# All stores of h on GpSimd, two h loads ahead of the last stores, and another order of splits at the head of a block

## The chip, the cores and the metric

The kernel runs on one core of one Trainium2 chip. The metric is the device time of one execution in microseconds. In the profile PE is TensorE, DVE is VectorE, ACT is ScalarE, POOL is GpSimd and SP is SyncE, which here only issues transfers.

## The reference

One decoder layer over 512 tokens of width 2048: two groups of attention heads, a cross attention to 256 memory tokens, and a SwiGLU. The change lies in the last part alone, with D_FF = 5632:

```python
hf = rms_norm(x, g_ffn)
gg, uu = jnp.split(hf @ w_gu, 2, axis=-1)
return x + (jax.nn.silu(gg) * uu) @ w_down
```

Below, h is `silu(gg) * uu`.

## The kernel before, in words

All matrix products run in fp32 accuracy on a reduced-precision matmul: each operand is split into a high part, a rounded copy (ScalarE, `S.copy`), and a low part, the rest (VectorE, `tensor_sub`), and a product is three matmuls (`mm3`: high x high, high x low, low x high). `split` (its line in the profile is L159 for both halves) is used for weights and activations alike. TensorE's matmuls are recorded on L99.

Both projections of the SwiGLU use a scheme with seven products instead of eight for a 2x2 block matrix, so weights and activations are also added and subtracted before they are split.

**Up projection.** Eleven blocks n of 512 columns of D_FF (`NB` = 11). In a block, phase 1 computes four of the products and phase 2 three; each phase goes over eight pairs of K tiles (kp = 0 to 7). For each kp, `weights_1` (phase 1) loads `raw` through SP, subtracts (L1288), splits the first 1024 columns ("a"), adds (L1290), keeps a copy of the sum in a `T4` tile (L1292), and splits the other 1024 columns ("b"). In phase 1 TensorE takes the products of pairs 0 and 1 first, product by product: the first two products use halves of b, the next two use a; then pair by pair. All splits are buffered in five `qh` and four `ql` tiles, the loads in three `raw` tiles.

**h.** When block n is done, h of block n-1 is turned while phase 2 of block n runs (`turn`): for each of two halves k, `blocks` transposes 32x32 squares on VectorE into one `T4` tile (L1390), `combine` adds and subtracts into a second (L1398 to L1401), and two `put` store them to HBM in runs of 128 bytes, eight DMAs each (L1410). So a block has 32 stores and uses four `T4` tiles, and there are four `T4` buffers. For blocks 0 to 9 all stores are issued by GpSimd. For the last block, 10, `turn` runs in step 0 of the down projection, and its stores are issued in turn by SP and by ScalarE:

```python
if step == 0 and kp in (2, 4):
    for i, go in enumerate(turn(hs, NB - 1, kp // 2 - 1)):
        go(*[(nc.sync, nc.scalar)] if i > 1 else [])
```

**Down projection.** Four steps with one or two products each; in a step 22 kp. h is loaded back through GpSimd (`load_h`, L1554) in six groups of two blocks (the last of one), into `PB` tiles, and split into two more `PB` tiles. There are 16 `PB` buffers; until the last phase 2 they hold the activations of the up projection and come free kp by kp. Group g serves kp 4g to 4g+3. In step 0, groups 0 to 3 are loaded ahead of the loop, group 4 is written at kp 5 and group 5 (block 10 alone) at kp 11; the loads of groups 2 and 3 wait for a chosen matmul of the last phase 2 (`gate`). Weights come through SP into `raw`, two kp at a time (`load_w`). In step 0 the residual x, stored before, is also loaded into `raw` and turned back by TensorE (`turn_x2`, L1622) behind the odd kp from 5 on; ScalarE copies it out of PSUM (L1625), half of it into two `T4` tiles for each of two halves.

**Order.** The program is written in one sequence; a scheduler makes from it one queue for each engine, by priorities (`high_priority` moves an instruction ahead by so many places, `AHEAD` = 150, `EVICT` = 170) and by what its own model says is ready. On the chip each engine then works its queue strictly in order. A DMA is an entry in the queue of the engine that issues it; where it must wait for a buffer or an earlier transfer, everything behind it in that queue waits too. Work handed to `phase` in `extra` is written behind the named kp of the phase.

Of the kernel before, what the change touches and what calls it, by code (L numbers as in the profile page):

```python
# [25 lines left out]
NB = D_FF // 512  # L26
# [34 lines left out]
def hybrid_block(ctx: ExitStack, tc: tile.TileContext, x_t, mem_t, sv, cmat, umask, w_a, w_r67, w_v, w_vg, w_v3,  # L61
# [94 lines left out]
    def split(hi, lo, src, gain=None):  # L156

        if gain is None:
            return S.copy(hi, src), V.tensor_sub(lo, src, hi)  # L159
        return (S.activation(hi, src, AF.Copy, scale=gain),  # L160
                V.scalar_tensor_tensor(lo, src, gain, hi, op0=OP.mult, op1=OP.subtract))
# [45 lines left out]
    def part(pair, a, n):  # L207
        return pair[0][:, a:a + n], pair[1][:, a:a + n]
# [879 lines left out]
    def sb1(tag, dt=F32):  # L1088
        return pool1.tile([128, COLS2.get(tag, 512)], dt, name=tag, tag=tag, bufs=BUFS2[tag])
# [7 lines left out]
    def split_cols(raw, a, n):  # L1097
        hi, lo = sb1("qh", F32R), sb1("ql", F32R)
        done_split[0] = split(hi[:, :n], lo[:, :n], raw[:, a:a + n])
        return hi, lo  # L1100
# [91 lines left out]
    def sb2(tag, dt=F32):  # L1192
        return pool2.tile([128, COLS2.get(tag, 512)], dt, name=tag, tag=tag, bufs=BUFS2[tag])
# [86 lines left out]
    def keep(kp):  # L1280
        if kp % 2 == 0:
            t = sb1("T4")
            kept[kp], kept[kp + 1] = t[:, :512], t[:, 512:]

    def weights_1(n, kp):
# [7 lines left out]
        b = split_cols(raw, 1024, 1024)  # L1293
        return part(b, 512, 512), part(b, 0, 512), part(a, 0, 512), part(a, 512, 512)

    def weights_2(n, kp):
        raw = sb1("raw")
        nc.sync.dma_start(raw[:, :1024], w_gu[n, kp, :, 0:1024])
        V.tensor_sub(raw[:, 1024:1536], raw[:, 0:512], kept[kp])
        a = split_cols(raw, 0, 1024)  # L1300
        b = split_cols(raw, 1024, 512)
        return part(a, 0, 512), part(b, 0, 512), part(a, 512, 512)
# [46 lines left out]
    PHASE_1 = (4, 0, 5, 3)  # L1349
    PHASE_2 = (1, 2, 6)  # L1350

    def phase(load, banks, plan, middle, last, fresh, ahead, extra, fence=()):

        ws = {}

        def weights(kp):
            with tc.high_priority(offset=AHEAD if kp > 1 else ahead), ExitStack() as behind:
                if kp == 2:
                    for i in fence:
                        behind.enter_context(tc.issue_after(i.ins))  # L1360
                ws[kp] = load(kp)

        for kp in range(2):
            weights(kp)
        for p, a in enumerate(plan):
            for kp in range(2):
                product(banks[p], kp, a, ws[kp][p], fresh and kp == 0, False, not fresh)
        for kp in range(2, KP):
            weights(kp)
            for p in last if kp == KP - 1 else middle:  # L1370
                product(banks[p], kp, plan[p], ws[kp][p], False, kp == KP - 1, not fresh)
            for go in extra.get(kp, ()):
                go()
# [77 lines left out]
    def late_sum():  # L1451
        return {kp: [sums.pop(0)] for kp in (3, 5)}

    rc2 = []
    gate = []
    hs = None
    fence = ()
    for n in range(NB):
        if n == 0:
            b1, bp = first_banks  # L1460
            u, c11 = [sb2("C") for _ in range(2)], [sb2("C") for _ in range(2)]
            with tc.high_priority(offset=2 * EVICT):
                for i in range(2):
                    fa = S.copy(u[i], b1[i])
                for i in range(2):
                    fv = V.tensor_add(c11[i], u[i], bp[i])
            bu, b2, b3 = [bank("mm"), bank("mm")], [bank("mm"), bank("o")], [bank("t"), bank("t")]

            def last_sums():
                with tc.high_priority(offset=AHEAD):  # L1470
                    with tc.issue_after(splits_b[1][0].ins), tc.issue_after(splits_b[1][1].ins):
                        form_sums(KP - 1)

            phase(lambda kp: weights_b(n, kp), (bu, b2, b3), (4, 5, 3), (1, 2, 0), (0, 1, 2), True, 40,
                  {2: [last_sums]}, (fa, fv))
        else:
            b1 = c11 = [bank("mm"), bank("mm")]
            bu = [bank("s"), bank("s")]
            b2 = [bank("t"), bank("t")]
            b3 = [bank("mm"), bank("o")]  # L1480
            phase(lambda kp: weights_1(n, kp), (bu, b1, b2, b3), PHASE_1, (2, 3, 1, 0), (1, 0, 2, 3), True, AHEAD, late_sum(),
                  fence)
            u = [sb2("C") for _ in range(2)]
        c22 = [sb2("C") for _ in range(2)]
        with tc.high_priority(offset=EVICT):
            for i in range(2):
                if n:
                    fa = S.copy(u[i], b1[i])
                V.tensor_add(u[i], u[i], bu[i])
            for i in range(2):  # L1490
                V.tensor_add(c22[i], u[i], b2[i])  # L1491
            for i in range(2):
                fv = V.tensor_add(c22[i], c22[i], b3[i])
        extra = {}
        if hs:
            one, two = [turn(hs, n - 1, k) for k in range(2)]
            extra = {2: [one[0]], 3: [one[1], one[2]], 4: [one[3]], 5: [two[0]], 6: [two[2], lambda: gate.append(last_mm[0])],
                     7: [two[1], two[3]]}
            if ready_made:
                extra[5] += [ready_made.pop(0), ready_made.pop(0)]  # L1500
        if n == 0:
            def scales():
                ss2 = sb2("C")
                G.dma_start(ss2, ssd)
                rc2.append(token_norm_col(ss, D, NT, ss2))

            phase(lambda kp: weights_c(n, kp), (b2, b3), (2, 6), (0, 1), (0, 1), False, AHEAD, {3: [scales]}, (fv,))
            rc2 = rc2[0]
        else:
            phase(lambda kp: weights_2(n, kp), (b1, b2, b3), PHASE_2, (1, 0, 2), (0, 1, 2), False, AHEAD, extra,  # L1510
                  (fa, fv))
        g1, g2 = [sb2("C") for _ in range(2)], [sb2("C") for _ in range(2)]
        with tc.high_priority(offset=EVICT):
            for i in range(2):
                fa = S.activation(g1[i], c11[i], AF.Silu, scale=rc2[:, i:i + 1])
            for i in range(2):
                V.tensor_add(g2[i], u[i], b2[i])  # L1517
            for i in range(2):
                fv = V.tensor_add(u[i], u[i], b3[i])
        fence = fa, fv  # L1520
        for i in range(2):
            S.activation(g2[i], g2[i], AF.Silu, scale=rc2[:, 2 + i:3 + i])
        for i in range(2):
            V.scalar_tensor_tensor(g1[i], u[i], rc2[:, i:i + 1], g1[i], op0=OP.mult, op1=OP.mult)
        for i in range(2):
            V.scalar_tensor_tensor(g2[i], c22[i], rc2[:, 2 + i:3 + i], g2[i], op0=OP.mult, op1=OP.mult)
        hs = g1 + g2

    STEPS = ((6,), (0, 3), (4, 5), (1, 2))
    quad = [(i, j) for i in range(2) for j in range(2)]
    groups, dw = {}, {}

    SPLIT_AT = {(1, 3): (1, 6)}
    for s in (1, 2, 3):
        SPLIT_AT[s, 4], SPLIT_AT[s, 5] = (s, 10), (s, 14)
        if s > 1:
            SPLIT_AT[s, 0], SPLIT_AT[s, 1], SPLIT_AT[s, 2], SPLIT_AT[s, 3] = (s - 1, 18), (s, 2), (s, 4), (s, 6)
    h_raw = {}  # L1540

    def split_h(step, g):
        n = 512 * len(GRP[g])
        for a in STEPS[step]:
            hi, lo = sb2("PB", F32R), sb2("PB", F32R)
            split(hi[:, :n], lo[:, :n], h_raw.pop((a, g))[:, :n])
            groups[a, g] = hi, lo

    def load_h(step, g):
        n = 512 * len(GRP[g])  # L1550
        for a in STEPS[step]:
            raw = h_raw[a, g] = sb2("PB")
            r = 128 * SLOT[a] - 128
            i = G.dma_start(raw[:, :n], hd[g][r:r + 128])  # L1554
            if step == 0 and g in (2, 3):
                tc.add_manual_dep(i.ins, gate[-1].ins.name,
                                  mybir.DependencyInfo(mybir.DependencyClass.Sync, mybir.DependencyReason.DATA),
                                  reason="in its turn")
        if (step, g) not in SPLIT_AT:
            split_h(step, g)  # L1560

    def late_splits(step, kp):
        for (s, g), at in SPLIT_AT.items():
# [87 lines left out]
    SETS = ("mm", "o", "t", "t"), ("s", "s", "mm", "mm")  # L1651
    banks = [None, [bank(t) for t in SETS[1]]]

    for g in range(len(GRP) - 2):
        load_h(0, g)
    for step, plan in enumerate(STEPS):
        rs_ = range(len(plan))
# [8 lines left out]
        for kp in range(NK):  # L1666
# [18 lines left out]
                        nc.sync.dma_start(raw, x2d[m // 4])  # L1685
                    turned[step, kp] = turn_x2(m, raw)
            if step == 0 and kp in (2, 4):
                for i, go in enumerate(turn(hs, NB - 1, kp // 2 - 1)):
                    go(*[(nc.sync, nc.scalar)] if i > 1 else [])
            if step == 0 and kp in (5, 11):  # L1690
                load_h(0, len(GRP) - (2 if kp == 5 else 1))
            if step < 3 and kp % 4 == 3:
# [139 lines left out]
```

## Time and profile before

| | |
|---|---|
| median of 3 timed runs | 2299.12 us (2298.78 to 2301.11) |
| profiled execution: its own time | 2295.67 us |
| its span, first to last instruction | 2293.6 us |
| granted TensorE clock, mean | 0.997 |
| up projection, blocks 1 to 10, one block | about 77 us |
| down projection | from 1845 us to the end |

Times within the profile are microseconds from the span's start. A row of the timeline is start, duration, engine, line, operation, output <- inputs, shapes, count, and in brackets the idle time before it and what ended that idle time. A row of the waits is engine, line and tensor <- what it waited for: microseconds in total, times, longest. A row of a window is its bounds and length, then for each engine the busy time and its instructions, then the granted clock, the busy share of the DMA engines and GB/s. A row of a DMA queue is packets, MB, and the share of 16 engines over the window; a row of DMA issues ends with KB each and the microseconds to landing.

### The profile page before, as it was taken

How to read it: one execution, taken by the hardware profiler on the slowest of the kernel's cores; microseconds unless marked ns; L12 is line 12 of the kernel's file. 1: busy time of each engine (PE TensorE's matmuls, PEld its weight loads, DVE VectorE, ACT ScalarE, POOL GpSimd, SP SyncE). 2: the span in 40 equal slices, each digit the busy share in tenths (PEclk: the TensorE clock that was granted, in tenths of full speed). 3: DMA queues.
4: the chain of work that ended last, by engine and by line, in shares of the span. 5: the costliest groups of instructions: out<-in, count | busy, mean ns of one | idle time of the engine just before them, and what ended most of it. 6: DMA issues, size and time to landing. Idle time of an engine off the chain costs nothing.

```text
span 2293.6 us, 29822 instructions
## 1 busy us (share of the span) xinstructions
PE 2264.0 (99%) x10597; PEld 1876.0 (82%) x10597; DVE 1687.8 (74%) x2643; ACT 1163.7 (51%) x1811; POOL 365.6 (16%) x560
## 2 busy tenths in 40 slices
PE   9999999999999999999999999999999979999999
PEld 7988888888888888787888888888888868888887
DVE  6478766677784446698888888988898856775685
ACT  6334545566774345675445444544454436444452
POOL 0012100011110000110223322332233220000000
PEclk9999999999999999999999999999999989999999
DMA  6577656466654334685556656665665588766754
GB/s 197 142 184 183 171 156 172 123 174 174 164 170 168 135 132 138 219 231 178 181 176 206 196 174 182 206 190 174 182 212 175 166 275 302 266 233 249 266 206 147
DMA packets 144565, 434.21 MB, mean 189 GB/s; under 512 B 33024, under 2 KB 34048, under 8 KB 140960
## 3 DMA queue, kind: packets, MB, share of 16 engines
q1 hardware_dynamic: 88176, 307.75, 39.7%
q0 software_dynamic: 44064, 115.12, 20.7%
q10 hardware_dynamic: 12176, 9.44, 1.3%
q8 instruction: 83, 1.36, 0.2%
q14 instruction: 66, 0.54, 0.1%
HBM read 390.81 MB, written 94.11 MB: 211 GB/s over the span
## 4 chain that ended last, share of the span: by engine, by line
PE 89%; DVE 5%; DMA 3%; issue 2%; ACT 1%; DVEq 0%; SPq 0%; POOL 0%; ACTq 0%
PE mm L99 49%; PE t L99 16%; PE s L99 14%; PE o L99 9%; DVE ql L159 2%; DMA raw<-w_gu 1%; PE t L817 1%; DMA h<-T 1%; DVE wl L159 1%; DMA raw<-w_down 0%; DVE C L1517 0%; ACT qh L159 0%; DMA w<-w_vsw 0%; DMA w<-w_c 0%; ACT wh L159 0%
## 5 line engine op out<-in xcount | busy, mean ns | idle before, releaser
L159 ACT CAST qh<-raw 128x1024 fp32r<-128x1024 f32 (+1 forms) x526 | 512.5, 981 | 523.1 <-PE o L99 143.4
L159 DVE TENSOR_TENSOR ql<-raw,qh 128x1024 fp32r<-128x1024 f32 (+1 forms) x526 | 589.0, 1128 | 142.1 <-PE mm L99 51.3
L99 PE MATMUL mm<-X,wh 128*128 128x512 f32 x1600 | 504.1, 395 | 0.0
L99 PEld LDWEIGHTS mm<-X,wh 128*128 128x128 f32 x1600 | 294.0, 188 | 56.4 <-issue 0.8
L99 PE MATMUL t<-qh,PB 128*128 128x512 f32 x968 | 333.4, 389 | 0.0
L99 PE MATMUL mm<-X,wl 128*128 128x512 f32 x800 | 313.6, 392 | 0.5 <-DVE wl L159 0.4
L99 PE MATMUL mm<-qh,PB 128*128 128x512 f32 x868 | 310.2, 390 | 1.8 <-DVE C L1491 0.9
L159 DVE TENSOR_TENSOR wl<-w,wh 128x1024 fp32r<-128x1024 f32 (+2 forms) x150 | 179.6, 1199 | 154.2 <-ACT wh L159 152.4
L159 ACT CAST wh<-w 128x1024 fp32r<-128x1024 f32 (+2 forms) x150 | 154.3, 1030 | 239.5 <-PE mm L99 179.5
L99 PE MATMUL s<-qh,PB 128*128 128x512 f32 x672 | 233.4, 392 | 14.4 <-ACT PB L159 14.3
L1410 POOL DMA_DIRECT2D h<-T x320 | 204.2, 708 | 217.1 <-DVE T L1390 174.4
L99 PE MATMUL mm<-qh,PA 128*128 128x512 f32 x640 | 221.4, 389 | 0.0
L99 PEld LDWEIGHTS t<-qh,PB 128*128 128x128 f32 x968 | 181.7, 188 | 38.1 <-ACT qh L159 0.2
L99 PEld LDWEIGHTS mm<-qh,PB 128*128 128x128 f32 x868 | 163.1, 188 | 37.1 <-ACT qh L159 2.1
L99 PE MATMUL t<-ql,PB 128*128 128x512 f32 x484 | 188.3, 389 | 0.0
L99 PE MATMUL o<-qh,PB 128*128 128x512 f32 x484 | 187.4, 389 | 0.0
L99 PEld LDWEIGHTS mm<-X,wl 128*128 128x128 f32 x800 | 150.3, 188 | 33.0 <-DVE wl L159 1.9
L99 PE MATMUL mm<-ql,PB 128*128 128x512 f32 x434 | 169.3, 390 | 0.0
L99 PEld LDWEIGHTS s<-qh,PB 128*128 128x128 f32 x672 | 126.4, 188 | 40.9 <-ACT PB L159 14.6
L99 PEld LDWEIGHTS mm<-qh,PA 128*128 128x128 f32 x640 | 120.1, 188 | 25.0
L99 PE MATMUL s<-ql,PB 128*128 128x512 f32 x336 | 132.7, 395 | 4.4 <-DVE ql L159 4.2
L99 PE MATMUL mm<-ql,PA 128*128 128x512 f32 x320 | 124.5, 389 | 0.0
(495 smaller groups left out, 3513.4 us busy)
## 6 DMA issues: line engine op xcount, KB each, us to landing
raw<-w_gu SPq DMA_DIRECT2D x88, 768.0 KB, 4.8
raw<-w_gu SPq DMA_DIRECT2D x88, 512.0 KB, 3.9
raw<-w_down SPq DMA_DIRECT2D x84, 512.0 KB, 4.7
td<-w_down POOLq DMA_DIRECT2D x66, 512.0 KB, 6.4
w<-w_a SPq DMA_DIRECT2D x60, 512.0 KB, 4.4
raw<-td SPq DMA_DIRECT2D x22, 1024.0 KB, 4.8
PB<-h POOLq DMA_DIRECT2D x35, 512.0 KB, 5.5
w<-w_out SPq DMA_DIRECT2D x32, 512.0 KB, 3.5
```

Source lines behind the costliest of these rows:

```text
L99: last_mm[0] = PE.matmul(*args, **kw)
L159: return S.copy(hi, src), V.tensor_sub(lo, src, hi)
L817: PE.transpose(tp[:, 128 * (i - j):128 * (i - j) + 128], ps_[b][:, POFF[i] + 128 * j:POFF[i] + 128 * j + 128], ident)
L1410: queues[i].dma_start(rows[:, :, c:c + 32], src[32 * q:32 * q + 32, :, i])
```

## The change

Three edits.

1. The stores of block 10 go through the default of `put`, GpSimd, as those of the other blocks do.
2. The loads and splits of h groups 0 and 1 for step 0 move from ahead of the down projection into phase 2 of the last block: group 0 ahead of the `combine` and the first store behind kp 3, group 1 ahead of the next `blocks` behind kp 5. The definitions of `load_h` and what it uses move up for that.
3. In blocks 1 to 10 the first two pairs of phase 1 are loaded and split by one new function: both loads, then for each pair the subtraction, the addition, the kept copy and the split of b, and only then the splits of a for both pairs.

```diff
+    def first_weights(n):
+        raws, a, b = [sb1("raw") for _ in range(2)], [], []
+        for kp, raw in enumerate(raws):
+            nc.sync.dma_start(raw[:, :1536], w_gu[n, kp, :, 512:2048])
+        for kp, raw in enumerate(raws):
+            V.tensor_sub(raw[:, 0:1024], raw[:, 0:1024], raw[:, 512:1536])
+            V.tensor_add(raw[:, 1536:2048], raw[:, 0:512], raw[:, 1024:1536])
+            keep(kp)
+            S.copy(kept[kp], raw[:, 1536:2048])
+            b.append(split_cols(raw, 1024, 1024))
+        for raw in raws:
+            a.append(split_cols(raw, 0, 1024))
+        return [(part(b[i], 512, 512), part(b[i], 0, 512), part(a[i], 0, 512), part(a[i], 512, 512)) for i in range(2)]
...
-        for kp in range(2):
-            weights(kp)
+        if both:
+            with tc.high_priority(offset=ahead):
+                ws.update(enumerate(both()))
+        else:
+            for kp in range(2):
+                weights(kp)
...
             phase(lambda kp: weights_1(n, kp), (bu, b1, b2, b3), PHASE_1, (2, 3, 1, 0), (1, 0, 2, 3), True, AHEAD, late_sum(),
-                  fence)
+                  fence, lambda: first_weights(n))
...
             extra = {2: [one[0]], 3: [one[1], one[2]], 4: [one[3]], 5: [two[0]], 6: [two[2], lambda: gate.append(last_mm[0])],
                      7: [two[1], two[3]]}
+            if n == NB - 1:
+                extra[3].insert(0, lambda: load_h(0, 0))
+                extra[5].insert(0, lambda: load_h(0, 1))
...
-    for g in range(len(GRP) - 2):
+    for g in range(2, len(GRP) - 2):
         load_h(0, g)
...
             if step == 0 and kp in (2, 4):
-                for i, go in enumerate(turn(hs, NB - 1, kp // 2 - 1)):
-                    go(*[(nc.sync, nc.scalar)] if i > 1 else [])
+                for go in turn(hs, NB - 1, kp // 2 - 1):
+                    go()
```

More of the change, by code (lines that the diff above doesn't have):

```diff
@@ L1350, in hybrid_block, with phase @@
     PHASE_2 = (1, 2, 6)
-    def phase(load, banks, plan, middle, last, fresh, ahead, extra, fence=()):
+    def phase(load, banks, plan, middle, last, fresh, ahead, extra, fence=(), both=None):
         ws = {}
@@ L1452, in late_sum, with split_h, load_h @@
         return {kp: [sums.pop(0)] for kp in (3, 5)}
+    STEPS = ((6,), (0, 3), (4, 5), (1, 2))
+    quad = [(i, j) for i in range(2) for j in range(2)]
+    groups, dw = {}, {}
+    SPLIT_AT = {(1, 3): (1, 6)}
+    for s in (1, 2, 3):
+        SPLIT_AT[s, 4], SPLIT_AT[s, 5] = (s, 10), (s, 14)
+        if s > 1:
+            SPLIT_AT[s, 0], SPLIT_AT[s, 1], SPLIT_AT[s, 2], SPLIT_AT[s, 3] = (s - 1, 18), (s, 2), (s, 4), (s, 6)
+    h_raw = {}
+    def split_h(step, g):
+        n = 512 * len(GRP[g])
+        for a in STEPS[step]:
+            hi, lo = sb2("PB", F32R), sb2("PB", F32R)
+            split(hi[:, :n], lo[:, :n], h_raw.pop((a, g))[:, :n])
+            groups[a, g] = hi, lo
+    def load_h(step, g):
+        n = 512 * len(GRP[g])
+        for a in STEPS[step]:
+            raw = h_raw[a, g] = sb2("PB")
+            r = 128 * SLOT[a] - 128
+            i = G.dma_start(raw[:, :n], hd[g][r:r + 128])
+            if step == 0 and g in (2, 3):
+                tc.add_manual_dep(i.ins, gate[-1].ins.name,
+                                  mybir.DependencyInfo(mybir.DependencyClass.Sync, mybir.DependencyReason.DATA),
+                                  reason="in its turn")
+        if (step, g) not in SPLIT_AT:
+            split_h(step, g)
     rc2 = []
@@ L1527, in hybrid_block @@
         hs = g1 + g2
[L1531 to L1560, printed above, removed]
     def late_splits(step, kp):
```

## The prediction

> **What bounds the kernel now.** First I read the page's totals, to see which engine fills the time:
>
> ```profile
> span 2293.6 us, 29822 instructions
> ...
> PE 2264.0 (99%) x10597; PEld 1876.0 (82%) x10597; DVE 1687.8 (74%) x2643; ACT 1163.7 (51%) x1811; POOL 365.6 (16%) x560
> ```
>
> TensorE (PE) is busy 99%, and the change adds or removes no matmul. What it can win are waits of PE; what it can lose are new ones. So next come PE's waits, from 1200 us to the end and then for 1100 to 1850 alone:
>
> ```profile
> PE s L99 <- ACT PB L159: 14.3, 1, 14.3
> PE s L99 <- DVE ql L159: 4.2, 8, 1.1
> ```
>
> ```profile
> PE s L99 <- DVE ql L159: 4.0, 7, 1.1
> ```
>
> So one long wait, for a ScalarE split of h, and seven short ones at the block boundaries (4.0 us together). PE's timeline shows where the long one lies:
>
> ```profile
> 1850.42 0.39 PE L99 MATMUL s<-qh,PB 128*128 128x512 f32 x1
> ...
> 1853.14 0.39 PE L99 MATMUL s<-qh,PB 128*128 128x512 f32 x1
> ...
> 1855.87 1.04 PE L1622 MATMUL t<-ident,raw 128*128 128x128 f32 x8
> 1871.23 0.79 PE L99 MATMUL s<-qh,PB 128*128 128x512 f32 x1 [14.33 <-ACT PB L159]
> ...
> 1875.99 0.40 PE L99 MATMUL s<-qh,PB 128*128 128x512 f32 x1
> ```
>
> Step 0 of the down projection takes 2.72 us for each kp (1850.42 to 1853.14, 12 matmuls). kp 0 to 3 use h group 0 and run; kp 4 needs group 1 and waits 14.33 us. The 12 matmuls from 1871.23 to 1875.99 then take 4.76 us, 2.04 more than 2.72. Why group 1 is late is seen in ScalarE's timeline, SP's, GpSimd's (POOL) and the chain of waits, in this order:
>
> ```profile
> 1856.96 13.13 ACTq L1410 DMA_DIRECT2D h<-T  x11
> 1870.14 1.04 ACT L159 CAST PB<-PB 128x1024 fp32r<-128x1024 f32 x1 [13.37 <-DMA h<-T]
> ```
>
> ```profile
> 1856.63 16.62 SPq L1410 DMA_DIRECT2D h<-T  x16
> 1873.34 0.46 SPq L1685 DMA_DIRECT2D raw<-x  x1
> ```
>
> ```profile
> 1822.16 0.64 POOL L1410 DMA_DIRECT2D h<-T  x1 [1.94 <-DVE T L1390]
> ...
> 1846.31 2.69 POOL L1410 DMA_DIRECT2D h<-T  x4 [1.09 <-DMA h<-T]
> 1849.47 0.57 POOL L1554 DMA_DIRECT2D PB<-h  x1 [0.47 <-issue]
> ```
>
> ```profile
> 1852.33 7.02 DMA raw<-w_down
> ...
> 1859.37 8.46 DMA h<-T
> ...
> 1867.85 2.30 DMA h<-T
> ```
>
> Group 1 was requested at 1849.47, behind block 9's 32 stores. But ScalarE, which must split it, stands from 1856.96 to 1870.14 in 11 stores of block 10's h, each held back by earlier transfers. The blocked ScalarE, not the data, holds PE.
>
> **The change part by part.**
>
> *Stores of block 10 go to POOL.* ScalarE loses 16 issues and SP 16. Group 1's load was issued at 1849.47 and lands by this row:
>
> ```profile
> PB<-h POOLq DMA_DIRECT2D x1, 512.0 KB, 6.5
> ```
>
> That is 1856.0; one cast (1.04) gives 1857.0, against 1856.9, when PE wants it. So this part alone recovers nearly all of the 14.33 us, and the 2.04 us of slow matmuls with it. SP is also free for the second x tile from 1856.63 instead of 1873.34.
>
> The price is on POOL. Each store costs there what these rows say (minimum, median, maximum ns):
>
> ```profile
> L1410 POOL DMA_DIRECT2D h<-T x320: 615/649/1107, 1129.8 to 1848.3; - x160
> ...
> L1410 SPq DMA_DIRECT2D h<-T x16: 302/346/515, 1856.6 to 1872.7; - x16
> ```
>
> 32 x 0.649 = 20.8 us of issue; with its waits, the set of block 9 took 1822.16 to 1849.00 = 26.8 us. VectorE's first transposes for block 10 end at 1856.93:
>
> ```profile
> 1855.84 1.09 DVE L1390 STREAM_TRANSPOSE T<-C 128x256 f32<-128x256 f32 x3
> ```
>
> So the last store is issued at about 1883.7 and has landed 4.2 us later (next row, the page's) at 1887.9:
>
> ```profile
> h<-T POOLq DMA_DIRECT2D x160, 64.0 KB, 4.2
> ```
>
> Queued behind the stores on POOL are h groups 4 and 5 of step 0. Group 5 needs all stores of block 10: 1887.9 + 6.5 + a split of under 2.3 = 1896.7; kp 20 wants it at 1856.9 + 16 x 2.72 + 7 x 1.04 (sets of transposes) = 1907.7. Hidden, with 11 us to spare. Group 4: 1883.7 + 6.5 + 2.3 = 1892.5 against kp 16 at 1856.9 + 12 x 2.72 + 5 x 1.04 = 1894.7. Hidden, by only 2 us; every microsecond beyond that would be PE's. Step 1's h loads behind them are wanted after 1907 and have more.
>
> On the DMA engines the POOL stores are no dearer: GpSimd's queue in 1745 to 1773, a stretch with 32 stores, and ScalarE's in 1845 to 1876, with 16:
>
> ```profile
> q0 software_dynamic: 975, 1.77, 25.1%
> ```
>
> ```profile
> q10 hardware_dynamic: 6889, 0.85, 18.7%
> ```
>
> 28 x 0.251 = 7.0 us of all engines for 32 against 31 x 0.187 = 5.8 us for 16.
>
> *What is late next.* Two waits come up once PE runs on. The first: the four T4 buffers. Block 10's stores read four T4 tiles, and the residual copies of the first x tile (kp 5) want two more, which must come free by stores landing. Before, VectorE met such a wait:
>
> ```profile
> 1868.41 0.43 DVE L1398 TENSOR_TENSOR T<-T 128x256 f32<-128x256 f32 x1 [7.71 <-DMA h<-T]
> ```
>
> On POOL the first two tiles are stored by 16 issues from 1856.93: 10.4 us at 0.649, 13.4 at the pace of block 9's set; plus 4.2 they free T4 at 1871.5 to 1874.5. PE's transposes of kp 7 come at 1856.9 + 4 x 2.72 = 1867.8 and need the PSUM banks that those copies empty. If the copies stand in ScalarE's queue for T4, PE waits 3.7 to 6.7 us, and the splits behind the copies with it; if other instructions are queued ahead, 0. The second: kp 10's weights need the raw buffer that the x tile holds until those transposes, as SP's own wait shows:
>
> ```profile
> SPq L1574 <- PE t L1622: 11.2, 1, 11.2
> ```
>
> The order of these two is the same before and after, and before it cost PE nothing that matters; only a slower landing does. w_down's landing was 4.8 us in 1878 to 1886, 8.2 in 1850 to 1857:
>
> ```profile
> raw<-w_down SPq DMA_DIRECT2D x2, 512.0 KB, 4.8
> ```
>
> ```profile
> raw<-w_down SPq DMA_DIRECT2D x2, 512.0 KB, 8.2
> ```
>
> So 0 to 3.4 us. A gap of PE also slows the matmuls after it, 0 to 2.04 us. Give-back: 0 to 6.7 + 3.4 + 2.0 = 12.1. I take 5.0, the middle of the T4 wait and nothing for the rest, since the nearest row is VectorE's 7.71 in the same place.
>
> The granted clock in that gap (column after the busy times):
>
> ```profile
> 1865.00:1870.00 5.00, 0.00 (x0) 0.00 (x0) 1.52 (x4) 0.00 (x0) 0.00 (x0) 0.50 0.77 123
> ```
>
> [...]
>
> *The first two h loads ahead of block 9's last stores.* Two POOL issues move ahead and push those stores by 2 x 0.57 = 1.1 us; nobody waits for them but group 4. Group 0 was split inside phase 2 already; new there is group 1's split, 1.04 us on ScalarE and some 1.2 on VectorE. Phase 2's last 30 us, and the following stretch, by engine:
>
> ```profile
> 1815.00:1845.00 30.00, 30.00 (x134) 24.82 (x134) 24.66 (x40) 15.36 (x19) 17.85 (x29) 1.00 0.80 249
> 1845.00:1876.00 31.00, 16.63 (x70) 13.05 (x69) 18.72 (x31) 9.35 (x16) 6.04 (x11) 0.78 0.99 275
> ```
>
> VectorE has 5.3 us idle and ScalarE 14.6 there; without that cover 1.2 us would be PE's. If the load lands late, weight splits queue behind the waiting cast, as they did for group 0:
>
> ```profile
> 1824.53 1.06 ACT L159 CAST PB<-PB 128x1024 fp32r<-128x1024 f32 x1 [1.80 <-DMA PB<-h]
> ```
>
> I count 0. Its gain is part of the 14.33 above: without it group 1's low half would come some 3 us late (the load at 1856.0, cast and subtraction one after the other behind other splits).
>
> *A block's first two pairs.* The same copies and subtractions in another order: both b tiles, which PE uses first, before both a tiles. At one boundary PE, VectorE and SP show:
>
> ```profile
> 1464.20 0.50 PE L99 MATMUL s<-ql,PB 128*128 128x512 f32 x1 [0.61 <-DVE ql L159]
> ```
>
> ```profile
> 1462.92 1.22 DVE L159 TENSOR_TENSOR ql<-raw,qh 128x1024 fp32r<-128x1024 f32 x1
> 1464.06 1.22 DVE L1288 TENSOR_TENSOR raw<-raw 128x1024 f32<-128x1024 f32 x1
> 1465.94 1.23 DVE L1288 TENSOR_TENSOR raw<-raw 128x1024 f32<-128x1024 f32 x1 [0.66 <-DMA raw<-w_gu]
> ```
>
> ```profile
> 1458.71 5.79 SPq L1287 DMA_DIRECT2D raw<-w_gu  x2
> ```
>
> PE waits for the second pair's b, last of the four subtractions. In the new order an a tile is last, wanted only after 24 matmuls on b (two kp's worth, 5.4 us). One place earlier in VectorE's queue is 1.22 us, more than the longest wait (1.1), so all 4.0 us go. Cost: the first raw buffer is freed up to two subtractions (2.5 us) later, so the load at 1458.71 and the subtraction at 1465.94 move to 1468.4; ahead of pair 3 PE does 8 products of 6 matmuls for pairs 0 and 1 and 24 matmuls for pair 2. At 1464.20 fewer than 24 of these 72 are done, so pair 3 is wanted after 1464.2 + 48 x 0.227 (2.72 / 12) = 1475.1, and 1468.4 plus three VectorE steps of 1.2 is 1472. Hidden, 3 us to spare.
>
> **Sum.** -14.3 - 2.0 - 4.0 + 5.0 = -15.3 us. The profiled execution took 2295.67 us (span 2293.6), the three timed runs 2299.12 in the median, 3.5 more. -15.3 gives 2280.4 against the first and 2284 against the median.
>
> **The rivals.**
> *Nothing is late next*: T4 and weights are there because the order of queues fits. -20.3, 2279. For it: blocks 1 to 9 store by POOL with no PE wait but the 4.0 us. Against: step 0 adds two T4 users and the x tiles.
> *The wait moves to kp 7 and 8*: the full give-back of 12.1, -8.2, 2291; for it the 7.71 us row. [...]
> *The change does not do what it says*: step 0's stall reforms because ScalarE waits as long for T4 as it did for its own stores, and only the 4.0 stays. Within 0.2%, 2295.
> *Slower*: the late release of the first raw buffer, at each of ten boundaries. To use up the spare 3 us and then the 15.3 and 4.6 shared by ten, 2.0 each, pair 3 must come 2.5 + 3 + 2.0 = 7.5 us later than now; I count 2.5. At 8.0 PE would lose 25 us, and the time would be 2309. Against it: VectorE's wait for that load is 0.66 now.
>
> **How the numbers follow.** Forecast 0.36, nothing late next 0.27, wait moved 0.18, not what it says 0.10, slower 0.09. A change under 0.2% (4.6 us) can't be told from none. Faster: 0.36 + 0.27 + 0.18 = 0.81; same 0.10; slower 0.09. The forecast's own range is 2279 to 2291; the range given, 2276 to 2297, takes in "nothing late next" with 3 us for a freer SP queue, the moved wait and the third rival at 2295, and leaves out the slower case and some of each edge.
>
> **What would show it.** PE's 14.3 us wait on the PB split gone; the seven boundary waits gone; a PE wait near 1868 of 0 to 7 us, on ScalarE's copies or a split; no store on ScalarE's or SP's queue; step 0 ending some 11 us earlier. Wrong: a PE wait over 8 us in step 0, PE waits inside phase 2 before 1845, or waits on pair 3 at the boundaries.

## The result, and the profile after

| | before | after |
|---|---|---|
| median of 5 runs each, side by side | 2299.12 us (2297.8 to 2301.11) | 2286.88 us (2285.18 to 2289.6) |
| ratio | | 0.9949, 95% interval 0.9938 to 0.9959 |
| profiled execution, and its span | 2295.67, 2293.6 us | 2286.88, 2285.1 us |

The change made the kernel faster by 12.2 us in the medians (forecast 15, to 2284) and by 8.8 us in the profiled executions, where the forecast's sum was -15.3. The profile of before was a quick execution, 3.5 us under its median; that of after lies on its median. So the time came out within 3 us of the forecast while the sum, against its own reference, was 6.5 us too large. The closeness is luck of the reference: timed a second time ("full change again" below), the change took 9.4 us off the median, so 10.8 in the mean of the two, nearer to the -8.2 of the rival "the wait moves" than to -15.3. What follows keeps to the profiles.

The totals of after, then PE's waits from 1200 us to the end (total, times, longest):

```profile
span 2285.1 us, 29869 instructions
...
PE 2266.0 (99%) x10597; PEld 1878.2 (82%) x10597; DVE 1689.3 (74%) x2643; ACT 1165.2 (51%) x1811; POOL 386.7 (17%) x592
```

```profile
PE t L1643 <- ACT T L1646: 4.0, 1, 4.0
PE mm L99 <- DVE ql L159: 1.8, 1, 1.8
PE s L99 <- DVE ql L159: 0.8, 1, 0.8
PE s L99 <- ACT qh L159: 0.7, 1, 0.7
PE mm L99 <- ACT qh L159: 0.3, 1, 0.3
```

The 14.3 us on a PB split and the waits at the boundaries from 1200 us on are gone. New are 4.0 us for ScalarE's copies into T4 and four waits for weights, 3.6 us together. That explains only a part of what is missing, so I cut PE's timeline at places that can be recognised in both kernels: block 1's first matmul into bank "s", the first one into "s" in its phase 2, step 0's first, the first one into "s" of step 1, and the last matmul. Before:

```profile
1076.23 0.62 PE L99 MATMUL s<-qh,PB 128*128 128x512 f32 x2
...
1091.43 0.39 PE L99 MATMUL s<-qh,PB 128*128 128x512 f32 x1
...
1844.98 0.39 PE L99 MATMUL s<-qh,PB 128*128 128x512 f32 x1
...
1934.78 0.39 PE L99 MATMUL s<-qh,PB 128*128 128x512 f32 x1
...
2289.15 0.39 PE L99 MATMUL t<-qh,PB 128*128 128x512 f32 x1
```

After:

```profile
1074.69 0.62 PE L99 MATMUL s<-qh,PB 128*128 128x512 f32 x2
...
1078.22 0.50 PE L99 MATMUL s<-ql,PB 128*128 128x512 f32 x1 [2.46 <-DVE ql L159]
...
1092.85 0.39 PE L99 MATMUL s<-qh,PB 128*128 128x512 f32 x1
...
1839.49 0.39 PE L99 MATMUL s<-qh,PB 128*128 128x512 f32 x1
...
1925.80 0.63 PE L99 MATMUL s<-qh,PB 128*128 128x512 f32 x1
...
2280.64 0.39 PE L99 MATMUL t<-qh,PB 128*128 128x512 f32 x1
```

| stretch | before | after | difference |
|---|---|---|---|
| up to block 1 (no edit there) | 1076.23 | 1074.69 | -1.54 |
| phase 1 of block 1 | 15.20 | 18.16 | +2.96 |
| from there to step 0 | 753.55 | 746.64 | -6.91 |
| step 0 and the head of step 1 | 89.80 | 86.31 | -3.49 |
| the rest | 354.37 | 354.84 | +0.47 |
| sum | | | -8.51 |

Two lines surprise. Block 1 loses 3 us, where the wait in the rows above is new. And step 0, which had 14.33 + 2.04 = 16.4 us to win, wins 3.5: it gave 12.9 us back. PE's timeline of step 0 shows where (only transposes and rows with a wait):

```profile
1855.82 1.03 PE L1643 MATMUL t<-ident,raw 128*128 128x128 f32 x8
1866.30 1.97 PE L1643 MATMUL t<-ident,raw 128*128 128x128 f32 x8 [3.99 <-ACT T L1646]
1875.63 1.03 PE L1643 MATMUL t<-ident,raw 128*128 128x128 f32 x8
...
1890.35 0.50 PE L99 MATMUL s<-qh,PB 128*128 128x512 f32 x1 [0.74 <-ACT qh L159]
1891.60 0.50 PE L99 MATMUL s<-ql,PB 128*128 128x512 f32 x1 [0.76 <-DVE ql L159]
...
1922.73 0.50 PE L99 MATMUL mm<-ql,PB 128*128 128x512 f32 x1 [1.82 <-DVE ql L159]
```

The same sets of transposes start in before at 1884.17, 1890.51 and, for the one behind the waits of 0.7 us (1897.03 in after), 1909.99. With step 0 starting 5.5 us earlier and 16.4 of stall gone, all should come 21.9 us earlier. They come 17.9, 14.9 and 13.0 earlier, and the first "s" of step 1 only 9.0. So the give-back is 4.0 (T4) + 3.0 (matmuls at half clock) + 1.9 (weights of kp 14) + 4.0 (weights at the head of step 1, again with half clock). The chain behind the first is in ScalarE's timeline:

```profile
1865.97 0.44 ACT L1646 COPY T<-t 128x128 f32<-128x128 f32 x2 [4.36 <-DMA h<-T]
```

The copy stands until a store of block 10 has landed and freed a T4 tile. The chain behind the weights is in another row of ScalarE and in the waits of SP's own queue from 1835 to 1930:

```profile
1889.24 1.05 ACT L159 CAST qh<-raw 128x1024 fp32r<-128x1024 f32 x1 [4.91 <-DMA raw<-w_down]
```

```profile
SPq L1595 <- PE t L1643: 19.2, 2, 15.9
...
SPq L1706 <- DMA raw<-w_down: 13.2, 3, 7.4
```

SP cannot start the next weights (L1595) until the transposes have released the raw buffer that an x tile holds: 19.2 us in two waits, 15.9 for the weights of kp 10 and 3.3 for those of kp 14, whose cast is the row above.

### The profile page after: what moved, and what is told of

It is laid out like the page before. It is cut to its first block, busy times and chain, and to the rows that moved or that the text cites. A ratio compares the mean times of both kernels' runs of the same rounds, so it can differ in the third digit from the quotient of the medians.

```text
span 2285.1 us, 29869 instructions
## 1 busy us (share of the span) xinstructions
PE 2266.0 (99%) x10597; PEld 1878.2 (82%) x10597; DVE 1689.3 (74%) x2643; ACT 1165.2 (51%) x1811; POOL 386.7 (17%) x592
## 4 chain that ended last, share of the span: by engine, by line
PE 93%; DMA 2%; DVE 2%; issue 1%; ACT 1%; POOL 0%; SPq 0%; DVEq 0%; ACTq 0%; POOLq 0%
PE mm L99 51%; PE t L99 17%; PE s L99 13%; PE o L99 10%; DMA raw<-w_down 1%; PE t L817 1%; DVE ql L159 1%; ACT qh L159 1%; DVE wl L159 0%; DMA w<-w_vsw 0%; DMA h<-T 0%; DMA w<-w_c 0%; ACT wh L159 0%; DMA P<-w_v 0%; POOL h L1428 0%
## 5 line engine op out<-in xcount | busy, mean ns | idle before, releaser
L1428 POOL DMA_DIRECT2D h<-T x352 | 224.9, 704 | 221.8 <-DVE T L1408 181.1
```

Source lines behind the costliest of these rows:

```text
L1428: queues[i].dma_start(rows[:, :, c:c + 32], src[32 * q:32 * q + 32, :, i])
```

## The experiments

All were timed in five rounds beside the kernel before. "Step 0" is the fourth stretch of the table above, from its profiled execution, "block 1" the second.

| kernel | median, us | ratio to before, 95% | block 1 | to step 0 | step 0 |
|---|---|---|---|---|---|
| edit 1 (stores) | 2292.68 | 0.9975 (0.9966 to 0.9985) | 14.96 | 754.86 | 87.62 |
| edit 2 (h loads) | 2295.52 | 0.9987 (0.9979 to 0.9996) | 14.96 | 753.98 | 88.09 |
| edit 3 (heads) | 2293.49 | 0.9973 (0.9963 to 0.9984) | 17.29 | 746.64 | 90.36 |
| edits 1 and 3 | 2288.93 | 0.9962 (0.9948 to 0.9975) | 17.41 | 746.64 | 85.92 |
| edits 1 and 2 | 2291.39 | 0.9981 (0.9973 to 0.9990) | 14.96 | 751.57 | 83.09 |
| full change again | 2286.16 | 0.9963 (0.9949 to 0.9976) | 16.69 | 746.64 | 85.68 |
| + residual in PA | 2290.93 | 0.9968 (0.9955 to 0.9981) | 17.23 | 746.64 | 90.02 |
| + block 1 old order | 2281.81 | 0.9936 (0.9923 to 0.9948) | 14.98 | 746.64 | 85.16 |
| + x tile in PA | 2283.78 | 0.9935 (0.9923 to 0.9948) | 16.82 | 746.64 | 80.39 |
| + x tile and residual in PA | 2289.19 | 0.9965 (0.9952 to 0.9977) | 17.53 | 746.64 | 87.75 |
| + block 1 old, x tile in PA | 2279.73 | 0.9933 (0.9921 to 0.9946) | 14.96 | 746.64 | 80.89 |
| + the same, x later | 2274.66 | 0.9915 (0.9901 to 0.9929) | 14.96 | 746.64 | 77.57 |

The rows came in three batches (the first three and "residual in PA"; then "edits 1 and 3" and the three from "block 1 old order" on; then the rest), each with its own runs of before, whose medians were 2298.03, 2297.87 and 2295.56. Two ratios of one batch compare best.

**Edit 1 alone**

```diff
-                for i, go in enumerate(turn(hs, NB - 1, kp // 2 - 1)):
-                    go(*[(nc.sync, nc.scalar)] if i > 1 else [])
+                for go in turn(hs, NB - 1, kp // 2 - 1):
+                    go()
```

> The kernel before with the first edit alone: block 10's stores on GpSimd; h loads and heads of blocks as before. Theory A (ScalarE stood in its own stores, so moving them frees PE): PE's 14.3 us wait on the PB split shrinks to 0 to 3 us, because group 1 is still loaded behind block 9's stores, and the T4 wait seen after the change comes in its place (PE 4 us on the transposes of the second x pair, then half clock for some 7 us). Against before -3 to -8 us. Theory B (group 1 was late because its load stood behind block 9's stores): the wait stays at 10 us or more, and the time is within 3 us of before. The eight boundary waits on ql (4.2 us) stay.

The time, 5.4 us under before in the medians, is theory A's. But of the 14.3 us 5.8 stay, where it had 0 to 3, and the T4 wait that it named does not come. What stays is two waits for group 1's split:

```profile
1860.20 0.50 PE L99 MATMUL s<-qh,PB 128*128 128x512 f32 x1 [1.47 <-ACT PB L159]
...
1865.21 1.22 PE L99 MATMUL s<-qh,PB 128*128 128x512 f32 x2 [4.28 <-DVE PB L159]
```

ScalarE's timeline and then VectorE's show why. Group 1's load, issued at 1848.75, has landed at about 1855.3 (an estimate, with the 6.5 us of the same load before), but ScalarE does four copies of x, behind PE's transposes, before the cast. The cast is done at 1860.2, and the subtraction, the low half, stands behind the transposes and combinations of block 10's h:

```profile
1858.33 0.87 ACT L1625 COPY PA<-t 128x128 f32<-128x128 f32 x4 [0.61 <-PE t L1622]
1859.09 1.06 ACT L159 CAST PB<-PB 128x1024 fp32r<-128x1024 f32 x1
```

```profile
1857.72 1.09 DVE L1390 STREAM_TRANSPOSE T<-C 128x256 f32<-128x256 f32 x3
...
1861.50 1.08 DVE L1390 STREAM_TRANSPOSE T<-C 128x256 f32<-128x256 f32 x3
...
1863.94 1.22 DVE L159 TENSOR_TENSOR PB<-PB 128x1024 fp32r<-128x1024 f32 x1
```

**Edit 3 alone** (`first_weights` for blocks 1 to 10, nothing else)

> The kernel before with the third edit alone: the new order of splits at the heads of blocks 1 to 10. Theory A: the seven boundary waits go and each later block is 76.16 us long, -6.9 us over blocks 1 to 9, but the first boundary (block 0 to 1) gets a wait of 2.5 us on ql, +3.0; so -4 us in all, and the 14.3 us wait of step 0 stays. Theory B (the block boundaries are worth what PE's waits say and nothing is lost at block 1): -4.0 us without a new wait near 1078. Rival C: the heads have no part in the gain, 0 us.

The stretch from block 1 to step 0 drops to 746.64, the same to the hundredth in every kernel that has the new order, and block 1 takes 2.1 us more. The long wait in step 0 stays (13.5 us on the PB split). With 4.5 us under before in the medians this is theory A, though the new wait near 1078 is 1.58 us here and not 2.5.

**Edit 2 alone** (h groups 0 and 1 loaded and split ahead of block 9's last stores; block 10's stores still by SP and ScalarE)

> The kernel before with the second edit alone: h groups 0 and 1 loaded and split inside the last phase 2; the stores of block 10 stay on SP and ScalarE. Theory A: group 1 is there in time, so PE runs kp 4 to 7 without the wait, but ScalarE still stands in its 16 stores until about 1870, with group 2's cast, the copies of x and the weight casts of kp 8 behind them; so the wait moves to kp 7 or 8 and is 5 to 10 us; -4 to -9 us against before. Theory B (the load's place was all that mattered): no wait over 2 us in step 0, -14 us or better, which would make the first edit idle.

The wait moved from the split to ScalarE's copies of x, at the transposes behind kp 7:

```profile
1879.31 1.12 PE L1643 MATMUL t<-ident,raw 128*128 128x128 f32 x4 [11.54 <-ACT T L1646]
```

ScalarE now stands in the same stores with the split already done, and what is late is the copy queued behind them:

```profile
1857.97 15.76 ACTq L1428 DMA_DIRECT2D h<-T  x11
```

The place is theory A's; the wait is longer than its 5 to 10 us, and the time only 2.5 us under before in the medians, not 4 to 9.

**Residual in PA**: the full change, with the first half's turned residual in four PA tiles and not in two T4.

```diff
-            t = [sb1("T4") for _ in range(2)]
-            res[1, b] = [t[x // 2][:, 512 * (x % 2):512 * (x % 2) + 512] for x in range(4)]
+            if b:
+                t = [sb1("T4") for _ in range(2)]
+                res[1, b] = [t[x // 2][:, 512 * (x % 2):512 * (x % 2) + 512] for x in range(4)]
+            else:
+                res[1, b] = [sb2("PA") for _ in range(4)]
```

> The changed kernel with one more edit: the first half of the residual's second two tiles goes into four PA tiles, free since the last phase 2, in place of two T4 tiles. Theory A (the 4.0 us wait of PE at the second x transposes is the T4 wait): that wait goes, the clock stays full there, and PE gains the 4.0 us and some 2.8 us of slow matmuls; -4 to -7 us against the changed kernel, about 2280 to 2283. Rival (the DMA engines are full there, 0.9 to 1.0 of their time, and weights come late anyway): the wait turns into one on the weights of kp 10, less than 2 us gained.

A miss: step 0 takes 90.02 us. The T4 wait at kp 7 is gone, but the other buffers also changed the scheduler's order, and the copies now come late elsewhere:

```profile
1901.30 1.97 PE L1646 MATMUL t<-ident,raw 128*128 128x128 f32 x8 [4.96 <-ACT T L1649]
```

ScalarE holds them behind casts that wait for w_down:

```profile
1897.74 1.04 ACT L159 CAST qh<-raw 128x1024 fp32r<-128x1024 f32 x1 [2.11 <-DMA raw<-w_down]
```

**Edits 1 and 3**: the full change without the loads ahead.

> Edits 1 and 3 without edit 2: h groups 0 and 1 are loaded behind block 9's stores, as before. Theory A (group 1's split is late by the 1.5 + 4.3 us that edit 1 alone showed, but this stands in for the 4.0 us T4 wait that the full change has at kp 7): the stores of edit 1 and the new order of edit 3 nearly add up, PE waits 4 to 6 us for a PB split near kp 4, none for T4, and the time is 1 to 3 us above the full change, a ratio to before of 0.9953 to 0.9962. Theory B (the loads ahead carry their weight, so that the split's lateness comes on top of the T4 wait): 5 to 7 us above the full change, 0.9970 to 0.9980. If the prediction was right that stores on GpSimd alone recover nearly all of the stall, the PB waits in step 0 are under 3 us.

PE waits 1.99 + 4.83 us for the PB split and nothing for T4; step 0 takes 85.92 us against 86.31 and 85.68 with the loads ahead. Theory A holds, at its edge (it had 4 to 6 us of waits for the PB split): 0.9962, beside 0.9949 and 0.9963 for the two measurements of the full change. Beside the other two edits the loads ahead are worth between nothing and 3 us, and these runs cannot tell which.

**Block 1 in the old order**

```diff
-                  fence, lambda: first_weights(n))
+                  fence, (lambda: first_weights(n)) if n > 1 else None)
```

> The full change, but block 1 takes its first two pairs in the old order; blocks 2 to 10 in the new one. Theory A (block 1's 3 us are lost because the subtraction of its second load now stands ahead of the first pair's halves in VectorE's queue, and this load comes late only there, behind the attention part): the 2.46 us wait near 1078 goes, the first matmul of block 1's phase 2 comes 2 to 3 us earlier, and the time is 2 to 3 us below the full change, a ratio to before of about 0.9938. Theory B (what block 1 loses now is not of the new order, or is taken back by block 2's boundary): within 1 us of the full change, 0.9949.

Theory A: the ratio is 0.9936, though the full change was not timed in this batch and its interval overlaps with this one. The trace is plainer: the wait of 2.46 us is gone and block 1 is back at 14.98:

```profile
1074.43 0.62 PE L99 MATMUL s<-qh,PB 128*128 128x512 f32 x2
...
1089.41 0.39 PE L99 MATMUL s<-qh,PB 128*128 128x512 f32 x1
```

VectorE in the full change shows what it was. The first pair's low half, wanted at once, stands behind the second pair's subtraction, which waits 2.25 us for its load, and then behind the evictions that follow it:

```profile
1073.42 1.23 DVE L1301 TENSOR_TENSOR raw<-raw 128x1024 f32<-128x1024 f32 x1 [2.25 <-DMA raw<-w_gu]
...
1076.95 1.22 DVE L159 TENSOR_TENSOR ql<-raw,qh 128x1024 fp32r<-128x1024 f32 x1
```

**x tile in PA**: four transfers of 256 KB into PA tiles.

```diff
-                        raw = sb1("raw")
-                        nc.sync.dma_start(raw, x2d[m // 4])
-                    turned[step, kp] = turn_x2(m, raw)
+                        xs = [sb2("PA") for _ in range(4)]
+                        for q in range(4):
+                            nc.sync.dma_start(xs[q], x2d[m // 4][:, 512 * q:512 * q + 512])
+                    turned[step, kp] = turn_x2(m, xs[m % 4])
```

> The full change, but each x tile is loaded into four PA tiles of 512 columns by four transfers of 256 KB and not into a raw buffer, so that the raw buffer stays with the weights. Theory A (the give-back behind kp 8 is the raw buffer that an x tile holds for 16 us of SP's queue): weights of kp 10 and later come in time, the waits of 0.7 + 1.8 us on their splits go, and the time is 3 to 5 us below the full change, a ratio of 0.9927 to 0.9936; the T4 wait of 4.0 us stays. Theory B (the DMA engines are full there, 0.87 to 1.0 busy, and set the pace whatever buffer waits): the same bytes land as late, the waits stay or move by under 1 us, and the ratio is 0.9945 to 0.9955.

Theory A. In PE's waits from 1835 to 1930 the weights are gone and T4 alone is left:

```profile
PE t L1642 <- ACT T L1645: 4.5, 1, 4.5
```

Step 0 falls by 5.9 us to 80.39. The DMA share and the traffic in that stretch are the same in both, first after, then this kernel (the three columns at the end are granted clock, DMA share and GB/s), so full DMA engines were not the cause:

```profile
1835.00:1930.00 95.00, 87.42 (x390) 70.35 (x389) 57.26 (x66) 51.29 (x106) 35.07 (x58) 0.95 0.89 310
```

```profile
1835.00:1930.00 95.00, 90.46 (x418) 74.90 (x417) 61.71 (x71) 53.67 (x109) 35.12 (x58) 0.96 0.89 309
```

**x tile and residual in PA** (both of the above edits)

> The full change, with both the x tiles and the first half's turned residual in PA tiles: neither a raw buffer for x nor the two T4 tiles for its first half. Theory A (the two buffers are separate causes of the give-back: T4 for 4.0 us of wait and some 2 us of slow matmuls, raw for the rest): all of step 0's waits go, 6 to 10 us below the full change, a ratio of 0.9905 to 0.9925. Theory B (full DMA engines set the pace behind kp 8): only the T4 part is gained, and half of it comes back as later waits for weights, as when the residual alone was moved: 0.9945 to 0.9970.

A miss again: 5.4 us slower than with the x tile alone, with new waits for PB splits (4.7 us) and for copies (3.3 us). Twice, then, step 0 grew when the residual was moved (90.02 us against 86.31, and 87.75 against 80.39). Which instruction of the changed order does it I did not settle.

**Edits 1 and 2**

> Edits 1 and 2 without edit 3. The new heads are worth the 4.0 us of boundary waits as PE's rows of before have them, and 4.5 us by edit 3 alone. Theory A (the boundaries and step 0 do not touch each other): the boundary waits are back, the T4 wait of about 4 us at kp 7 stays as in the full change, and the time is 4 to 5 us above the full change on the same chip, a ratio to before of 0.9965 to 0.9972. Theory B (the loads ahead carry little of their own): the time is that of edit 1 alone, 0.9975, within 1 us, since the T4 wait has taken the place of the late split. The two differ by the worth of edit 2 beside edit 1: 0 to 2 us.

On the same chip 5.2 us above the full change in the medians, and the T4 wait is there (4.2 us): theory A, though the ratio of 0.9981 lies above the figures of both theories. Edit 3 keeps its worth beside the others. Against edit 1 alone (0.9981 and 0.9975, other chips, intervals that overlap) the loads ahead show no gain. This kernel's profiled execution was the quickest of its 11 (2285.71), so its short step 0 in the table does not stand for its median.

**Block 1 in the old order and x tile in PA**

> Block 1's first pairs in the old order and the x tiles in PA tiles, together. Theory A (two places, two causes): the two gains add, 3 us for block 1 and 3 to 6 for the x tiles, so 6 to 9 us below the full change, a ratio to before of 0.9910 to 0.9923; the T4 wait of 4 us stays. Theory B (an earlier step 0 meets the same arrival of weights, so that a part of block 1's gain is waited away): 4 us below the full change, 0.9932.

6.4 us below the full change on the same chip: theory A, two places, two causes. (The ratio of 0.9933 alone would read as B, but on this chip the full change itself stood at 0.9963.)

**x later**: as the last, with

```diff
-            if step == 0 and kp % 2 and 5 <= kp < 21:
-                for m in (kp - 5, kp - 4):
+            if step == 0 and 9 <= kp < 17:
+                for m in (2 * kp - 18, 2 * kp - 17):
```

> As the one with block 1's old order and x in PA tiles, and the residual's transposes come behind kp 9 to 16, one pair after each, and not behind the odd kp from 5 to 19: the first is some 8 us later in PE's order, when the first stores of block 10 have landed and freed T4. Theory A (the T4 wait costs its 4 us and the slow matmuls behind it 2 us more): no wait on ScalarE's copies, 4 to 6 us below the kernel without this, a ratio of 0.9885 to 0.9905. Theory B (PE that runs on meets the next late thing, a split of group 2 or 3 or weights): a new wait of 2 to 5 us between kp 8 and 16 and a ratio within 0.9905 to 0.9930.

Both theories hold in part. The T4 wait is gone, step 0 takes 3.3 us less and the median is 5.1 us lower, as theory A has it. In its place PE waits for group 2's split at kp 8 (96 matmuls, eight kp, lie ahead of it), 1.5 + 0.7 us, the next late thing of theory B. PE's waits from 1835 to 1930:

```profile
PE s L99 <- ACT PB L159: 1.5, 1, 1.5
PE s L99 <- DVE PB L159: 0.7, 1, 0.7
PE t L1642 <- DMA PA<-x: 0.3, 1, 0.3
```

This version is the fastest: 0.9915 (0.9901 to 0.9929), 11.5 us below the full change on the same chip and 20.9 below the kernel before.

## Why the prediction was right, and where it was not

- **The blocked ScalarE held PE: right.** Without its stores on ScalarE the 14.3 us wait does not come back in any kernel; with them (edit 2 alone) it stays at 11.5 us, whatever the split does.
- **"This part alone recovers nearly all": wrong.** Edit 1 alone won 0.25%, and 1.47 + 4.28 us of waits stayed. The step that failed is the arithmetic after the landing, one cast of 1.04 us. It left out what stood ahead in both queues: in ScalarE's the copies of x, so that the cast began at 1859.09, some 3.8 us after the landing (estimated at 1848.75 + 6.5), and in VectorE's block 10's transposes, which held the subtraction until 1863.94. Without the loads ahead the low half was put 3 us late; it was 5.8, and 6.8 in edits 1 and 3.
- **The T4 wait: right.** Forecast at 3.7 to 6.7 us near 1868, it was 3.99 at 1866.30 (2.9 to 5.0 in the other runs that had it), by the store that the forecast named.
- **The other give-backs, taken as nothing: wrong, and here the sum failed.** Weights were bounded at 3.4 us and cost about 6: the x tile in PA returned 5.9 (5.3 against the second trace of the full change). The forecast saw that the raw buffer is held, but let only the landing be slower. It did not follow the delay on to the head of step 1, where 4 of the 6 us were lost. The slow matmuls were bounded at 2.0 and cost 3.0 (the granted clock was 0.52 from 1865 to 1872, row in the last section). In step 0 the rival "the wait moves to kp 7 and 8" (12.1 us) is what happened: 12.9.
- **GpSimd as the better place for the stores: not shown.** Before, half of the stores were on ScalarE, and what cost was ScalarE standing in them (13.13 us for 11 of them); without them on ScalarE edit 1 alone came to 0.9975. All 32 stores on SP's queue would have freed ScalarE too; no run here tried that.
- **The heads, -4.0: right in sum, by luck: two errors cancel.** PE's rows of waits showed 4.0 us at seven heads; the nine heads of blocks 2 to 10 gave 6.9 (4.9 to 8.2 against the other three traces with the old order). Such a row counts from the end of the matmul before, which lasts 0.39 us, while matmuls start every 0.227; counted from start to start, all nine heads were late before, 6.6 us together. The 3 us spare for pair 3 held: no wait at any later boundary, so the slower rival fell. But block 1's order was taken to be free. Its second load arrives after the first halves are wanted, and that cost 1.7 to 3.2 us against the 14.96 of the old order.
- **POOL's queue, groups 4 and 5 behind the stores: right.** PE never waits for them, though the forecast left group 4 only 2 us.

## What to carry to other kernels

When a long stall goes, list everything that was late behind it: here 14 us of waiting had hidden at least three, the low half of group 1, the T4 tiles and the raw buffer of the x tile, and an edit for one did not cure the others. A wait removed from a queue is worth the distance to the next late thing on any engine that feeds the same matmul, the second half of a split included. And a new order that helps at nine places can hurt at the tenth, where a load that it now waits for first is the late one; so look at each place where the code runs.

## What the runs showed of the hardware

Gaps far shorter than the 14.33 us of before brought half clock too. The granted clock of after in windows around two of them (length, busy times, clock, DMA share, GB/s):

```profile
1865.00:1872.00 7.00, 5.71 (x17) 4.55 (x18) 4.40 (x4) 5.66 (x14) 6.58 (x11) 0.52 0.90 244
...
1923.00:1926.50 3.50, 3.50 (x10) 2.73 (x10) 2.77 (x3) 0.41 (x1) 0.00 (x0) 0.55 0.99 387
```

A gap of 3.99 us brought 6.8 us at half clock, one of 1.82 us brought 3.4, and one of 2.46 us (block 1) none (1.00 from 1075 to 1088); in the fastest version 1.47 and 0.67 us close together brought 3.4. Each of these lengths is one or two times 3.4 us.

The length of one gap does not decide alone. Besides the 2.46 us that brought none and the 1.82 us that brought 3.4, in edit 1 alone gaps of 0.83 and 0.76 us, 1.26 us from the end of one to the end of the other, were followed by 3.4 us in which matmuls start every 0.42 to 0.43 us and not every 0.227, and in edits 1 and 2 a gap of 1.58 us brought none (1.00 from 1910 to 1930). What decides is not shown by these runs.
